# A two-layer hybrid decoder on one core: small fp32 products issued in groups, HGRN's score rows kept twice

## The chip, the cores and the metric

The kernel runs on one core of a Trainium2 chip. The metric is device time in microseconds (us) of one execution, the median over runs. Engines are named as in the profile: PE is TensorE, with PEld its weight loads, DVE is VectorE, ACT is ScalarE, POOL is GpSimd, SP is SyncE.

## The reference

One inference step of a decoder with two layers, width 1024, over 512 prompt tokens and 8 sequences of 8 sample tokens, all in fp32. A layer normalises `x`, projects it with one matrix (1024 to 2820 columns), and feeds four mixers of 256 columns each:

- SSD: a Mamba-2 mixer with 4 heads, 2 groups, state 64, and a short convolution ahead of it
- attention over a sliding window of 128 with sinks and a relative bias, 4 heads on 2 KV heads
- HGRN2: gated linear attention, 4 heads of 64 by 64
- RG-LRU: a gated linear recurrence with a convolution

```python
mix = concat([y_ssd, y_swa, y_hg, y_lru])
x = x + mix @ w_out
x = x + square(relu(rmsnorm(x) @ w_up)) @ w_down
```

The step returns the normalised `x` and all new caches and states of both groups.

## The kernel before

Activations lie transposed, features on partitions and all 576 tokens on the free axis. The big products (projections `pi`, output projection `pd`, MLP `pu`, `p`, `pd`, `pl`) split each fp32 operand into a high and a low fp32r part and run three matmuls of 128 by 128 by 288 where one would do in exact arithmetic. They stand on lines 339, 1102 and 1255. Each takes three of the eight PSUM banks (`mm`); all small products share the other five (`mx`, function `bank`).

Inside the mixers the products are small and plain fp32. One of these is issued as two matmul instructions, a transpose as one. The trace gives the part of the array that an instruction uses, as 128\*128 or 128\*64. The small products that matter here are these:

- `sc` and `scs` (lines 554 and 568): the scores of HGRN. Within a chunk of 128 tokens they are built level by level, for half lengths 1, 2, 4 up to 64 (`LEVELS`). A level scales rows of keys into `kE` and of queries into `qE` on DVE, multiplies them on PE (four `sc` for the prompt; one `scs` for the samples in the three shortest levels), and copies what its mask allows into `A` with two predicated copies for each bank. `kE` and `qE` are one buffer each. `hgrn` runs twice in each layer, for two pairs of heads.
- `dtt` (line 685): fifteen small transposes of SSD's dt values into one bank.
- `su` and `sus` (lines 781 and 793): SSD's state updates, four for the prompt's chunks and one for the samples, for each of two groups.
- `pts` (line 954): eight transposes of the sample tokens' attention weights.
- `lg`, `pt`, `ao` (lines 978, 1002, 354): the four prompt blocks of attention. A block computes scores (`lg`, four products), adds bias and takes the maximum on DVE, takes exponentials on ACT, and then, head by head, scales a row on ACT and transposes it (`pt`; 4 in the first block, 8 in the others). Two heads share a bank, which ACT copies into `PT`. The values follow (`ao`, 4 products in the first block, 8 in the others).

The four blocks are generators with three steps (scores, softmax, transposes and values), run by `staggered`, so that scores of a block are traced ahead of the transposes of the block before.

The order on each engine is set when the kernel is built: a scheduler walks the traced instructions, puts those first that were traced first among those ready by its own estimates, and raises marked ones (weight splits, what empties PSUM) over all others. `issue_after(ins)` adds an order edge on one engine and no semaphore. Each engine then works through its queue in that order. While a mixer's chain is on DVE and ACT, PE is given big products of what was traced later: projections of the next mixer, then the output projection, which for its first half (`outproj(0)`) needs HGRN and SSD, for its second (`outproj(1)`) LRU and attention.

Of the kernel before, what the change touches and what calls it, by code (L numbers as in the profile page):

```python
# [2 lines left out]

# [10 lines left out]
AF = mybir.ActivationFunctionType  # L14
# [121 lines left out]


def staggered(parts):

    n = 0  # L140
    while parts:
        n += 1
        for p in parts[:n]:
            if next(p, True):
                parts.remove(p)
                n -= 1


class Kern:
# [205 lines left out]

    def silu(self, out, in_):
        return self.nc.scalar.activation(out, in_, AF.Silu)
# [123 lines left out]
    def hgrn_begin(self):  # L481
# [3 lines left out]
        self.kE = P.t("kE")  # L485
        self.qE = P.t("qE", [2, TH])
        for t in (self.A, self.kE, self.qE):
            self.nc.gpsimd.memset(t, 0.0)
# [6 lines left out]
    def hgrn(self, p):  # L495
        nc, V, S, li, P = self.nc, self.nc.vector, self.nc.scalar, self.li, self.hp
        A, kE, qE = self.A, self.kE, self.qE
# [34 lines left out]

        for n, h in enumerate(LEVELS):
            W = T if h <= 4 else NP_
# [16 lines left out]
            ps = self.bank("sc")  # L551
            pv = ps.rearrange("p (d n) -> p d n", d=2)
            for ci in range(4):
                nc.tensor.matmul(pv[:, :, 64 * ci : 64 * ci + 64], kE[:, 128 * ci : 128 * ci + 128],  # L554
                                 qE[:, :, 64 * ci : 64 * ci + 64], start=True, stop=True)

            def into(rows, c0, c1, m, ps):
                w = (c1 - c0) // (2 * h)
# [4 lines left out]

            into(128, 0, NP_, self.lmask[:, n], pv)
            if h <= 4:
                ps = self.bank("scs")
                pv = ps[:64, :64].rearrange("p (d n) -> p d n", d=2)
                nc.tensor.matmul(pv, kE[:, NP_:T], qE[:, :, 256:288], start=True, stop=True)
                into(64, NP_, T, self.lmask[:64, n, :32], pv)
# [80 lines left out]
    def ssd_dt(self):  # L650
# [30 lines left out]
        pv = p2[:, :60].rearrange("p (c w h) -> p c w h", c=5, w=3)  # L681
        for ci in range(5):
            n = 128 if ci < 4 else NS
            for w, t in enumerate((dt, ac, ed)):
                nc.tensor.transpose(pv[:n, ci, w], t[:, 128 * ci : 128 * ci + n], self.ident[:4, :4])
# [16 lines left out]
    def ssd(self):  # L702
# [34 lines left out]
        for g in range(2):  # L737
# [39 lines left out]

            for ci in range(4):
                a = slice(128 * ci, 128 * ci + 128)
                pu = self.bank("su")  # L780
                nc.tensor.matmul(pu[rg, :128], Bt[:, 128 * ci + 64 * g : 128 * ci + 64 * g + 64], xd[:, a], start=True, stop=True)
# [6 lines left out]
            S0 = P.t("S0", [NB, 64])  # L788
# [606 lines left out]
```

## Time and profile before

| | |
|---|---|
| Median of 3 runs | 1359.47 us (1356.86, 1359.47, 1362.58) |
| The profiled execution | 1355.2 us |
| Its span on the core | 1353.4 us |
| Busy share of PE, DVE, ACT, POOL | 98%, 76%, 49%, 5% |
| Chain that ended last, by engine | PE 86%, DVE 7%, ACT 3%, issue 2% |
| Granted clock of PE, mean over the span | 0.998 |

The span runs from the first to the last instruction of the program; the execution's own time has 1.8 us around it. Times within the span are counted from its start. The mixers of the first layer lie between 0 and some 272 us, its MLP from there to 680, the second layer behind it. A matmul's end in the trace is modelled and matmuls overlap in the array, so that what one costs is read from the distance between starts, not from its duration.

### The profile page before, as it was taken

To read this page: it belongs to the slowest core of one execution; us is meant where nothing else is said; L and a number is where in the kernel's file an instruction comes from. 1 tells how busy PE (TensorE), PEld (TensorE's weight loads), DVE (VectorE), ACT (ScalarE), POOL (GpSimd) and SP (SyncE) were. 2 spreads that over 40 slices of the span, in tenths; PEclk is the share of its full clock that TensorE was granted. 3 is DMA by queue.
4 is the path that set the end of the run, shared out by engine and by line. 5 is a ranking of instruction groups with operands and counts; after the bars stand their busy time and mean duration, and the time that the engine had idled before them with its cause. 6 is when DMAs were issued, how large, how long until landed. Compare 5 with 4: busy or idle time off the path is not lost.

```text
span 1353.4 us, 25452 instructions
## 1 busy us (share of the span) xinstructions
PE 1328.0 (98%) x10384; PEld 1279.6 (95%) x10384; DVE 1028.5 (76%) x2043; ACT 658.2 (49%) x1175; POOL 63.3 (5%) x126
## 2 busy tenths in 40 slices
PE   7999999999999999999999999999999999999997
PEld 7999899799999999999999998988999999999997
DVE  7788888488678677776669678886977677777755
ACT  6565436766243334333354774477653243334325
POOL 2201102000000000000000001100000000000000
PEclk9999999999999999999999999999999999999999
DMA  6324414123213222322331233231223213222312
GB/s 237 104 87 139 165 68 144 48 79 110 77 65 110 78 92 81 113 75 86 131 121 47 98 117 128 94 111 48 79 81 123 78 63 109 79 82 91 115 58 71
DMA packets 39831, 131.36 MB, mean 97 GB/s; under 512 B 6089, under 2 KB 8241, under 8 KB 39681
## 3 DMA queue, kind: packets, MB, share of 16 engines
q1 hardware_dynamic: 29312, 102.12, 21.9%
q0 software_dynamic: 6512, 22.64, 5.0%
q10 hardware_dynamic: 3888, 4.97, 1.2%
q8 instruction: 82, 1.34, 0.4%
q14 instruction: 37, 0.30, 0.1%
HBM read 120.32 MB, written 11.34 MB: 97 GB/s over the span
## 4 chain that ended last, share of the span: by engine, by line
PE 86%; DVE 7%; ACT 3%; issue 2%; DMA 0%; SPq 0%; DVEq 0%; ACTq 0%
PE pd L339 33%; PE p L1102 21%; PE pi L339 15%; PE pu L339 6%; PE pl L1255 2%; PE sc L554 2%; DVE lo L326 1%; DVE a L444 1%; PE ss L402 1%; PE ao L354 1%; ACT hi L326 1%; DVE A L562 1%; DVE qE L550 1%; PE y L354 1%; PE lg L978 1%
## 5 line engine op out<-in xcount | busy, mean ns | idle before, releaser
L326 ACT CAST hi<-raw 128x1024 fp32r<-128x1024 f32 x134 | 140.2, 1046 | 297.1 <-PE pd L339 144.6
L339 PE MATMUL pd<-fh,hi 128*128 128x288 f32 x960 | 284.1, 296 | 0.0
L339 PE MATMUL pd<-fl,hi 128*128 128x288 f32 x960 | 284.0, 296 | 0.0
L339 PE MATMUL pd<-fh,lo 128*128 128x288 f32 x960 | 282.8, 295 | 0.0
L339 PE MATMUL pi<-xh,hi 128*128 128x288 f32 x704 | 210.6, 300 | 7.6 <-ACT xh L377 7.1
L339 PE MATMUL pi<-xl,hi 128*128 128x288 f32 x704 | 210.4, 300 | 1.1 <-DVE xl L378 1.1
L339 PE MATMUL pi<-xh,lo 128*128 128x288 f32 x704 | 211.1, 300 | 0.0
L326 DVE TENSOR_TENSOR lo<-raw,hi 128x1024 fp32r<-128x1024 f32 x134 | 163.6, 1222 | 27.3 <-ACT hi L326 26.7
L1037 DVE TENSOR_TENSOR x<-x,pd 128x288 f32<-128x288 f32 x240 | 108.2, 451 | 97.9 <-PE pd L339 97.8
L339 PEld LDWEIGHTS pd<-fh,lo 128*128 128x128 f32 x960 | 180.9, 188 | 0.0
L339 PEld LDWEIGHTS pd<-fh,hi 128*128 128x128 f32 x960 | 180.4, 188 | 0.0
L339 PEld LDWEIGHTS pd<-fl,hi 128*128 128x128 f32 x960 | 180.4, 188 | 0.0
L339 PEld LDWEIGHTS pi<-xh,hi 128*128 128x128 f32 x704 | 133.0, 189 | 10.1 <-ACT xh L377 7.1
L339 PEld LDWEIGHTS pi<-xh,lo 128*128 128x128 f32 x704 | 132.9, 189 | 6.0 <-issue 5.2
L339 PEld LDWEIGHTS pi<-xl,hi 128*128 128x128 f32 x704 | 132.9, 189 | 3.6 <-DVE xl L378 1.7
L1102 PE MATMUL p<-Th,ul 128*128 128x288 f32 x312 | 92.2, 296 | 0.0
L1102 PE MATMUL p<-Tl,uh 128*128 128x288 f32 x312 | 92.1, 295 | 0.0
L1102 PE MATMUL p<-Th,uh 128*128 128x288 f32 x312 | 92.0, 295 | 0.0
L1102 PE MATMUL p<-xl,uh 128*128 128x288 f32 x312 | 91.9, 295 | 0.0
L1102 PE MATMUL p<-xh,ul 128*128 128x288 f32 x312 | 91.9, 295 | 0.0
L1102 PE MATMUL p<-xh,uh 128*128 128x288 f32 x312 | 91.7, 294 | 0.0
L1078 ACT CAST uh<-raw 128x1024 fp32r<-128x1024 f32 x52 | 54.5, 1048 | 66.8 <-PE p L1102 43.2
(489 smaller groups left out, 3003.2 us busy)
## 6 DMA issues: line engine op xcount, KB each, us to landing
raw<-in_wu SPq DMA_DIRECT2D x64, 512.0 KB, 3.3
raw<-in_wd SPq DMA_DIRECT2D x64, 512.0 KB, 4.2
raw<-in_wi SPq DMA_DIRECT2D x44, 512.0 KB, 3.3
raw<-in_wo SPq DMA_DIRECT2D x16, 512.0 KB, 3.2
x<-in_xT SPq DMA_DIRECT2D x8, 288.0 KB, 5.9
a<-acd ACTq DMA_DIRECT2D x4, 576.0 KB, 4.5
xl<-in_xT POOLq DMA_DIRECT2D x8, 288.0 KB, 4.3
xd<-x POOLq DMA_DIRECT2D x8, 288.0 KB, 2.4
```

Of the source, the lines that this page charges most:

```text
L326: self.split_ins = nc.scalar.copy(hi, raw).ins, nc.vector.tensor_tensor(lo, raw, hi.bitcast(F32), op=ALU.subtract).ins
L339: self.nc.tensor.matmul(out, w, x[:, a], start=n == 0, stop=n == last)
L354: self.nc.tensor.matmul(out, w, x, start=n < 2, stop=n >= len(products) - 2, skip_group_check=True)
L402: nc.tensor.matmul(ps[:, :TH], ones, s[:, TH * h : TH * h + TH], start=n == 0, stop=n == len(sqs) - 1)
L444: V.scalar_tensor_tensor(dst[:, :CW], src[:, k : k + CW], w(k), dst[:, :CW], op0=ALU.mult, op1=ALU.add)
L550: V.tensor_tensor(qE[r, d, : W // 2].rearrange("p (n h) -> p n h", h=h), qu[r], eu[r], op=ALU.mult)
L554: nc.tensor.matmul(pv[:, :, 64 * ci : 64 * ci + 64], kE[:, 128 * ci : 128 * ci + 128], qE[:, :, 64 * ci : 64 * ci + 64], start=True, stop= ...
L562: V.copy_predicated(Av[:, d], m, ps[:, d].rearrange("p (n h) -> p n h", h=h))
L1037: self.nc.vector.tensor_tensor(y[:, a], x[:, a], ps, op=ALU.add)
L1078: S.copy(hl[0], src)
L1102: nc.tensor.matmul(ps[:, :TH], u, x, start=j == 0, stop=j == 11)
L1255: nc.tensor.matmul(ps, u[:, o + q], v[:, a], start=j == 0, stop=j == 11)
```

## The change

Instructions are regrouped; the arithmetic stays as it is. A helper, `together`, issues a list of products and puts an order edge from the first one to all the others on PE. The list is turned round, so that the first is one whose input is traced last. The 15 `dtt`, the 8 `pts` and each block's `pt` go through it.

HGRN gets two buffers each of `kE` and `qE`, all cleared at the start. Levels are held in pairs and a pair's products are issued together, the later level first; the seventh level stands alone. The predicated copies follow for both.

In SSD the samples' update `sus`, with its state load and the spreading of B by sequence ahead of it, moves in front of the four `su`, which stand behind it by an order edge.

In attention the blocks are four plain functions in a written order instead of generators. All four heads are scaled before the block's transposes. The values of a block are traced after the transposes of the next block and behind the first of these by an order edge; so are the scores of the block after the next. `PT` has four buffers instead of three, since a block's two live longer.

```diff
 
+    def together(self, calls):
+
+        first = calls[0]().ins
+        with self.tc.issue_after(first):
+            for c in calls[1:]:
+                c()
+        return first
...
         self.A = P.t("A", [2, T])
-        self.kE = P.t("kE")
-        self.qE = P.t("qE", [2, TH])
-        for t in (self.A, self.kE, self.qE):
+        self.kE = [P.t("kE", bufs=2) for i in range(2)]
+        self.qE = [P.t("qE", [2, TH], bufs=2) for i in range(2)]
+        for t in (self.A, *self.kE, *self.qE):
             self.nc.gpsimd.memset(t, 0.0)
...
 
+        held = []
         for n, h in enumerate(LEVELS):
+            kE, qE = self.kE[n % 2], self.qE[n % 2]
...
                 V.tensor_tensor(qE[r, d, : W // 2].rearrange("p (n h) -> p n h", h=h), qu[r], eu[r], op=ALU.mult)
-            ps = self.bank("sc")
-            pv = ps.rearrange("p (d n) -> p d n", d=2)
-            for ci in range(4):
-                nc.tensor.matmul(pv[:, :, 64 * ci : 64 * ci + 64], kE[:, 128 * ci : 128 * ci + 128],
-                                 qE[:, :, 64 * ci : 64 * ci + 64], start=True, stop=True)
-
-            def into(rows, c0, c1, m, ps):
-                w = (c1 - c0) // (2 * h)
+            held.append((n, h, kE, qE))
+            if n % 2 == 0 and h < LEVELS[-1]:
+                continue
+
+            first, banks = None, []
+            for n, h, kE, qE in held[::-1]:
+                ps = self.bank("sc")
+                banks.append((128, 0, NP_, h, self.lmask[:, n], ps.rearrange("p (d n) -> p d n", d=2)))
+                pv = banks[-1][-1]
+                for ci in range(4):
+                    with self.tc.issue_after(first) if first else nullcontext():
+                        ins = nc.tensor.matmul(pv[:, :, 64 * ci : 64 * ci + 64], kE[:, 128 * ci : 128 * ci + 128],
+                                               qE[:, :, 64 * ci : 64 * ci + 64], start=True, stop=True).ins
+                    first = first or ins
+                if h <= 4:
+                    ps = self.bank("scs")
+                    banks.append((64, NP_, T, h, self.lmask[:64, n, :32], ps[:64, :64].rearrange("p (d n) -> p d n", d=2)))
+                    with self.tc.issue_after(first):
+                        nc.tensor.matmul(banks[-1][-1], kE[:, NP_:T], qE[:, :, 256:288], start=True, stop=True)
+            held = []
+            for rows, c0, c1, h, m, ps in banks:
                 m = m.rearrange("p (n h) -> p n h", h=h)
                 Av = A[:rows, :, c0:c1].rearrange("p d (n u h) -> p d n u h", u=2, h=h)[:, :, :, 1]
                 for d in range(2):
                     V.copy_predicated(Av[:, d], m, ps[:, d].rearrange("p (n h) -> p n h", h=h))
-
-            into(128, 0, NP_, self.lmask[:, n], pv)
-            if h <= 4:
-                ps = self.bank("scs")
-                pv = ps[:64, :64].rearrange("p (d n) -> p d n", d=2)
-                nc.tensor.matmul(pv, kE[:, NP_:T], qE[:, :, 256:288], start=True, stop=True)
-                into(64, NP_, T, self.lmask[:64, n, :32], pv)
...
         pv = p2[:, :60].rearrange("p (c w h) -> p c w h", c=5, w=3)
+        calls = []
         for ci in range(5):
             n = 128 if ci < 4 else NS
             for w, t in enumerate((dt, ac, ed)):
-                nc.tensor.transpose(pv[:n, ci, w], t[:, 128 * ci : 128 * ci + n], self.ident[:4, :4])
+                calls.append(partial(nc.tensor.transpose, pv[:n, ci, w], t[:, 128 * ci : 128 * ci + n], self.ident[:4, :4]))
+        self.together(calls[::-1])
...
 
+            S0 = P.t("S0", [NB, 64])
+            self.dma(S0, self.I["sS0"][li, :, g])
+            ve = P.t("b", SLOT, bufs=2)
+            self.by_sequence(ve, Bt[:64, NP_ + 64 * g : NP_ + 64 * g + 64])
+            ps = self.bank("sus")
+            first = nc.tensor.matmul(ps, xd[:64, NP_:640], ve[:64, :512], start=True, stop=True).ins
             for ci in range(4):
                 a = slice(128 * ci, 128 * ci + 128)
                 pu = self.bank("su")
-                nc.tensor.matmul(pu[rg, :128], Bt[:, 128 * ci + 64 * g : 128 * ci + 64 * g + 64], xd[:, a], start=True, stop=True)
+                with self.tc.issue_after(first):
+                    nc.tensor.matmul(pu[rg, :128], Bt[:, 128 * ci + 64 * g : 128 * ci + 64 * g + 64], xd[:, a], start=True, stop=True)
                 if ci == 0:
                     V.tensor_copy(new[ci][rg], pu[rg, :128].rearrange("p (j n) -> p j n", j=2))
                     continue
                 for j in range(2):
                     V.scalar_tensor_tensor(new[ci][rg, j], new[ci - 1][rg, j], self.el[rg, j, ci : ci + 1],
                                            pu[rg, 64 * j : 64 * j + 64], op0=ALU.mult, op1=ALU.add)
-            S0 = P.t("S0", [NB, 64])
-            self.dma(S0, self.I["sS0"][li, :, g])
-            ve = P.t("b", SLOT, bufs=2)
-            self.by_sequence(ve, Bt[:64, NP_ + 64 * g : NP_ + 64 * g + 64])
-            ps = self.bank("sus")
-            nc.tensor.matmul(ps, xd[:64, NP_:640], ve[:64, :512], start=True, stop=True)
...
                 S.activation(l, l, AF.Copy, scale=sm[:, i, u : u + 1])
-        pc, pn = P.t("PT", [2, 256], bufs=3), P.t("PT", [2, 256], bufs=3)
-        for dst, rows, a in ((pc, 128, slice(0, 128)), (pn, 64, slice(128, 192))):
-            ps = self.bank("pts")
-            for k in range(4):
-                nc.tensor.transpose(ps[:rows, 128 * k : 128 * k + 128], Ls[k // 2][:, k % 2, a], self.ident)
+        pc, pn = P.t("PT", [2, 256], bufs=4), P.t("PT", [2, 256], bufs=4)
+        parts = [(self.bank("pts"), *x) for x in ((pc, 128, slice(0, 128)), (pn, 64, slice(128, 192)))]
+        self.together([partial(nc.tensor.transpose, ps[:rows, 128 * k : 128 * k + 128], Ls[k // 2][:, k % 2, a], self.ident)
+                       for ps, dst, rows, a in parts for k in (3, 2, 1, 0)])
+        for ps, dst, rows, a in parts:
             S.copy(dst[:rows].rearrange("p a n -> p (a n)"), ps[:rows])
...
 
-        def block(nb):
+        def scores(nb, behind=None):
             s0, n = (128 * (nb - 1), 256) if nb else (0, 128)
-            nk = n // 128
             a = slice(128 * nb, 128 * nb + 128)
             L = [P.t("L", [2, 256], bufs=4) for _ in range(2)]
-            mx, sm, ng = (self.small([128, 4], c) for c in ("mx", "sm", "ng"))
+            mx = self.small([128, 4], "mx")
             lg = [self.bank("lg").rearrange("p (e n) -> p e n", e=2) for i in range(2)]
-            for e in range(2):
-                for i in range(2):
-                    nc.tensor.matmul(lg[i][:, e, :n], Q[e][kv(i), a], K[kv(i), s0 : s0 + n], start=True, stop=True)
+            with self.tc.issue_after(behind) if behind else nullcontext():
+                for e in range(2):
+                    for i in range(2):
+                        nc.tensor.matmul(lg[i][:, e, :n], Q[e][kv(i), a], K[kv(i), s0 : s0 + n], start=True, stop=True)
             for i in range(2):
                 for e in range(2):
                     h = 2 * i + e
                     V.tensor_tensor_reduce(out=L[i][:, e, :n], in0=lg[i][:, e, :n], in1=bias[:, h, 256 - n :], scale=1.0,
                                            scalar=sinks[:, h : h + 1], op0=ALU.add, op1=ALU.max, accum_out=mx[:, h : h + 1])
-            yield
+            return L, mx, s0, n, a
+
+        def softmax(L, mx, s0, n, a):
+            sm, ng = (self.small([128, 4], c) for c in ("sm", "ng"))
             V.tensor_scalar(ng, mx, -1.0, None, op0=ALU.mult)
...
             V.tensor_tensor(sm, sm, mx, op=ALU.add)
             V.reciprocal(sm, sm)
-            yield
-            PT = [P.t("PT", [2, 256], bufs=3) for _ in range(2)]
-            for i in range(2):
-                pt = self.bank("pt").rearrange("p (e n) -> p e n", e=2)
-                for e in range(2):
-                    h = 2 * i + e
-                    l = L[i][:, e, :n]
-                    S.activation(l, l, AF.Copy, scale=sm[:, h : h + 1])
-                    for k in range(nk):
-                        nc.tensor.transpose(pt[:, e, 128 * k : 128 * k + 128], l[:, 128 * k : 128 * k + 128], self.ident)
-                S.copy(PT[i][:, :, :n], pt[:, :, :n])
+            for h in range(4):
+                l = L[h // 2][:, h % 2, :n]
+                S.activation(l, l, AF.Copy, scale=sm[:, h : h + 1])
+
+        def turned(L, mx, s0, n, a):
+            PT = [P.t("PT", [2, 256], bufs=4) for _ in range(2)]
+            pt = [self.bank("pt").rearrange("p (e n) -> p e n", e=2) for i in range(2)]
+            first = self.together([partial(nc.tensor.transpose, pt[i][:, e, 128 * k : 128 * k + 128],
+                                           L[i][:, e, 128 * k : 128 * k + 128], self.ident)
+                                   for i in (1, 0) for e in (1, 0) for k in range(n // 128)])
+            for i in (1, 0):
+                S.copy(PT[i][:, :, :n], pt[i][:, :, :n])
+            return first, PT
+
+        def values(PT, s0, n, a, behind=None):
             po = self.bank("ao").rearrange("p (e n) -> p e n", e=2)[:, :, :128]
             at = lambda i, k: s0 + 128 * k + 64 * i
-            self.tiled([(po[kv(i), e], vt[:, at(i, k) : at(i, k) + 64], PT[i][:, e, 128 * k : 128 * k + 128])
-                        for k in range(nk) for e in range(2) for i in range(2)])
+            with self.tc.issue_after(behind) if behind else nullcontext():
+                self.tiled([(po[kv(i), e], vt[:, at(i, k) : at(i, k) + 64], PT[i][:, e, 128 * k : 128 * k + 128])
+                            for k in range(n // 128) for e in range(2) for i in range(2)])
             S.copy(oh[:, :, a], po)
             V.tensor_tensor(ol[:, :, a], po, oh.bitcast(F32)[:, :, a], op=ALU.subtract)
 
-        staggered([block(nb) for nb in range(4)])
+
+        blocks = [scores(0), scores(1)]
+        softmax(*blocks[0])
+        old = None
+        for nb in range(4):
+            first, PT = turned(*blocks[nb])
+            if old:
+                values(*old, first)
+            if nb < 3:
+                softmax(*blocks[nb + 1])
+            if nb < 2:
+                blocks.append(scores(nb + 2, first))
+            old = PT, *blocks[nb][2:]
+        values(*old)
```

## Rows read from the trace of the kernel before

**Rows 1.** The page, busy time: engine, us busy, share of the span, instructions.

```profile
PE 1328.0 (98%) x10384; PEld 1279.6 (95%) x10384; DVE 1028.5 (76%) x2043; ACT 658.2 (49%) x1175; POOL 63.3 (5%) x126
```

**Rows 2.** Busy time by stretch: stretch, its length, engines' busy time, PEclk, DMA.

```profile
302.50:689.80 387.30, 387.30 (x2919) 387.06 (x2918) 287.61 (x519) 155.56 (x260) 8.73 (x16) 1.00 0.28 96
243.84:271.71 27.87, 26.62 (x199) 21.77 (x197) 14.39 (x58) 21.27 (x67) 0.00 (x0) 1.00 0.11 39
```

**Rows 3.** Waits of PE, whole span: us in total, times, longest us.

```profile
PE pts L954 <- ACT L L949: 1.6, 2, 1.3
PE pt L1002 <- ACT L L1000: 1.6, 2, 0.8
```

**Rows 4.** Timeline of PE, one short HGRN level, layer 1: start us, us, operation.

```profile
837.60 0.29 PE L339 MATMUL pi<-xh,lo 128*128 128x288 f32 x1
837.81 1.13 PE L554 MATMUL sc<-qE,kE 128*128 128x128 f32 x8
838.87 0.33 PE L568 MATMUL scs<-qE,kE 128*64 128x64 f32 x2
839.13 0.40 PE L339 MATMUL pi<-xh,hi 128*128 128x288 f32 x1
839.37 0.29 PE L339 MATMUL pi<-xl,hi 128*128 128x288 f32 x1
```

**Rows 5.** Timeline of PE, attention's prompt blocks, layer 0.

```profile
250.21 0.28 PE L1002 MATMUL pt<-cst,L 128*128 128x128 f32 x1
...
250.46 0.29 PE L1002 MATMUL pt<-cst,L 128*128 128x128 f32 x1
...
250.81 0.43 PE L354 MATMUL ao<-PT,vt 128*64 128x128 f32 x2
...
253.44 0.66 PE L1002 MATMUL pt<-cst,L 128*128 128x128 f32 x4
...
254.20 0.60 PE L1002 MATMUL pt<-cst,L 128*128 128x128 f32 x4
254.76 0.43 PE L354 MATMUL ao<-PT,vt 128*64 128x128 f32 x2
255.13 0.40 PE L339 MATMUL pd<-mixh,hi 128*128 128x288 f32 x1
255.46 0.70 PE L978 MATMUL lg<-x,x 64*128 64x256 f32 x2
256.08 1.09 PE L354 MATMUL ao<-PT,vt 128*64 128x128 f32 x14
257.10 1.13 PE L978 MATMUL lg<-x,x 64*128 64x256 f32 x6
258.16 0.40 PE L339 MATMUL pd<-mixl,hi 128*128 128x288 f32 x1
```

**Rows 6.** Timeline of PE, SSD's states, layer 1.

```profile
792.45 0.29 PE L339 MATMUL pi<-xl,hi 128*128 128x288 f32 x1
792.67 1.09 PE L781 MATMUL su<-c,Bt 128*64 128x128 f32 x8
793.69 0.40 PE L339 MATMUL pi<-xh,lo 128*128 128x288 f32 x1
...
795.08 1.12 PE L793 MATMUL sus<-b,c 64*128 64x512 f32 x2
796.13 0.40 PE L339 MATMUL pi<-xh,lo 128*128 128x288 f32 x1
```

**Rows 7.** Timeline of PE, a dt transpose, layer 1.

```profile
762.05 0.22 PE L685 MATMUL dtt<-cst,b 4*128 4x4 f32 x1
762.20 0.40 PE L339 MATMUL pi<-xh,hi 128*128 128x288 f32 x1
```

**Rows 8.** Timeline of POOL, the start.

```profile
1.74 0.58 POOL L488 MEMSET kE<- 128x576 f32 x1
...
11.86 0.84 POOL L208 COPY gate<-x 128x1 f32<-128x1 f32 x1 [8.52 <-DMA x<-in_xT]
```

More of the change, by code (lines that the diff above doesn't have):

```diff
@@ L2 @@
 from contextlib import ExitStack, nullcontext
+from functools import partial
 import numpy as np
@@ L135, in seqs @@
     return t[:, o : o + NB * w].rearrange("p (b t) -> p b t", b=NB)
[L138 to L146, printed above, removed]
 class Kern:
@@ L496, in hgrn @@
         nc, V, S, li, P = self.nc, self.nc.vector, self.nc.scalar, self.li, self.hp
-        A, kE, qE = self.A, self.kE, self.qE
+        A = self.A
         f, v, q, g = self.hin
```

## The prediction

> **What bounds the kernel.** I read the page first: TensorE is busy 98% of the span [rows 1]. A busy TensorE says little, since its matmuls overlap, so the next view is busy time by stretch. In the MLP of the first layer 2919 big products take 387.30 us, 0.1327 us from one start to the next, at a granted clock of 1.00 [rows 2]; nothing there is edited. In the four prompt blocks of the first layer's attention the same engine is busy 26.62 of 27.87 us, while ScalarE is busy 21.27 [rows 2]. The view of waits then shows how little of this is waiting: 1.6 us in all before the sample transposes (`pts`) and 1.6 us before the prompt transposes (`pt`), both for ScalarE's scaled rows [rows 3]. So the kernel is TensorE's issue stream from end to end. An edit is worth what it takes out of that stream, as long as the chain of softmax work does not turn the time into waits. The timeline shows where the stream is bad: not in the number of fp32 products, which is the same after, but in what one costs beside its neighbours. I read it by start-to-start distances and not by durations, because the ends are modelled.
>
> **The price of a neighbour.** One fp32 product is two instructions, called halves here; a transpose is one. A lone transpose between two big products: from one `pt` to the next is 0.25 us with one big product between them [rows 5], less 0.13 for the big one, 0.12. Four in a row take 0.56 us up to the next kind, 0.14 each, with the change of shape at their end in it [rows 5]. Both work on the tile 128\*128, as the big products do. Where the shape changes it is dear: `su` (tile 128\*64) starts 0.22 us after the last big product, its last half holds the next big product back [rows 6], and the big product after an `scs` needs 0.24 instead of 0.13 until its successor starts [rows 4]. So a group of another shape costs about 0.09 at its entry and 0.11 at its exit, and its own first and last halves are stretched too.
>
> The Trainium skill, TensorEngine Tiling (Array Packing), Key Properties, states it as a rule: a change of tiling mode drains TensorE, a change of tile alone does not. The trace agrees: 0.12 us for the lone transpose in the same mode, 0.22 us of entry into another mode. The rule speaks against a good part of this edit, since transposes (`pt`, `pts`) and the HGRN scores (`sc`) have the mode of the big products; by it their grouping is worth nothing, and without it, at the drain's price for each group, some 7 us more would be had.
>
> **The change part by part.**
>
> *Attention, prompt blocks.* The same 28 transposes, 56 value halves and 32 score halves a layer. Grouping the transposes gains nothing by the lone price; I take 0, bounds 0 and 0.5 us in all. What it brings is that the values of a block no longer stand behind the copies of their own block, half of which are late. Before, a burst goes two value halves, one big product, two score halves, fourteen value halves, six score halves: 3.40 us from 254.76 to 258.16 [rows 5], 3.27 without the big product. Unbroken, sixteen value halves cost the 1.02 of fourteen plus one step of about 0.11, and eight score halves the 1.06 of six plus about 0.21 (over a sixth of it, since the two halves of a pair start together), 2.40 together; fully paired, without the odd half at each end, 2.08. The gain is 0.87 to 1.19; I take 1.0. The first block's burst of eight and eight takes 2.63 [rows 5]; the same pieces unbroken make 0.65 (eight at the 0.073 of the fourteen and a longer first step) and 1.27, gain 0.7, or 1.0 paired; I take 0.8. Each occurs once in each layer: 3.6 us. In three of the other four blocks the values are broken only by big products, as two, a big one, fourteen: 0.37 for two halves that cost 0.11 in a run and 0.33 for a big product that costs 0.13 [rows 5], 0.46 lost, 1.4 us for three. Attention together 5.0, bounds 3.5 and 6.5.
>
> *HGRN scores.* Seven levels become four groups, in four calls: twelve groups fewer. A short level (`sc` and `scs`) costs 1.77 us from the last big product before it to the second behind it [rows 4], 1.50 without two big ones. In a pair, the second loses its entry (0.21 against 0.13: 0.08) and an exit (0.11), but `scs` now stands before an `sc`, and the way back into 128\*128 costs about 0.05 more than in a run: 0.13. Pairs with one `scs` or none save the entry alone, 0.08. Per call 0.13 + 0.08 + 0.08, for four calls 1.2 us; bounds 0 (the shape changes are as many) and 2.3 (entry and exit for all twelve). The vector work is unchanged. A level's rows wait for the pair before last instead of the last level, but DVE then stops behind both levels' scores at once; the big projections that fill TensorE meanwhile hide this, and without them it would cost DVE some 1 us a pair.
>
> *SSD states.* `su` costs 0.22 + 1.02 + 0.24 less two big ones, 1.21; `sus` 0.22 + 1.05 + 0.24 − 0.27 = 1.24 [rows 4, 6]. Joined, one entry and one exit: 2.26, gain 0.19. Four of these, and in one the four `su` are split today, about 0.3 more: 1.0 us, bounds 0.4 and 1.4. The state load and DVE's spreading of B move ahead; the same instructions, and DVE is not the bound here.
>
> *dt transposes.* Lone, one costs 0.22 + 0.15 + 0.24 − 0.27 = 0.34 [rows 4, 6, 7], in a run I put it at 0.06, under half of its own 0.15. Four stand apart today, two of them beside other fp32 products: 0.9 us, bounds 0 and 1.1.
>
> *Rows kept twice.* Two more clears of 0.58 us on POOL a layer [rows 8]. In the first, POOL sits idle 8.52 us before the gate copy [rows 8], which hides them; without that they would delay the first loads by 1.2. Two copies of the larger buffers move addresses; I count 0.
>
> The sum is 5.0 + 1.2 + 1.0 + 0.9 = 8.1 us, bounds 3.9 and 11.3.
>
> **What comes back as waits.** The first of each group is the one that is ready last: ten groups of transposes (two `pts`, eight `pt`) now stand on TensorE's queue behind the scaling of all heads, and everything behind them stands too: other transposes, the last block's values, the next scores, the big products. Today such waits add up to 3.2 us in four [rows 3]. Values a block late also make the output projection's second half begin a block later. Below, waits could vanish (−3.2); above, ten of the longest of either kind, 1.3 us [rows 3], 13. I take 2.0 more than today, about one wait of 0.8 to 1.3 in each layer. ScalarE sets a floor: 21.27 us of work in the stage, 6.6 below its length [rows 2], so a gain of 2.5 in it fits.
>
> 8.1 − 2.0 = 6.1 us from the profiled execution's 1355.2 us (span 1353.4 and 1.8 around it) gives 1349.1. The median of the three runs is 1359.47, 4.3 above that execution, so the forecast for a median is 1353.4 us.
>
> **The rivals.**
>
> *The softmax chain takes it.* TensorE saves 8.1 but waits for ScalarE nearly as long. For it: every idle stretch of TensorE in attention ends on ScalarE [rows 3], which is busy for three quarters of the stage [rows 2]. Against: it also waits for TensorE's broken bursts, which end sooner. With waits of 5 to 8 us: 1356.5 to 1359.5. Chance 0.23.
>
> *Slower.* The place is the head of each transpose group. It decides from 0.8 us of wait per group (ten of these are the 8.1). At 1.3, the longest today, the sum is 13 − 8.1 = 4.9 more, 1364.4; at 1.6, 1367.4. For it: both kinds of wait exist today with only one or two heads awaited. Against: the scheduler has big products to put ahead. Chance 0.12, two thirds of it past the bound below.
>
> *Any group costs, whatever its shape.* Then 35 fewer groups (18 `pt`, 5 `pts`, 12 `sc`) save more: at the 0.08 of a late entry 2.8, at a full entry and exit of 0.20 7.0: 1350.6 to 1346.4; vanished waits lead the same way. For it: lone products often show the 0.21 entry [rows 4]. Against: the lone transpose at 0.12. By the page's rule named above it would not happen. Chance 0.20.
>
> *The change does not do what it says.* An order edge puts the rest behind the first, not next to it; big products may still come between. Then only the dt and SSD parts count: about 1357.6. Against: the big products near these groups are traced later and so rank lower. Chance 0.05.
>
> **How the numbers follow.** The forecast, 1350.5 to 1356.5, has 0.40. What a measurement of this kernel can tell from no change is about 0.5%, 6.8 us: faster means under 1352.7, slower over 1366.3. Half the forecast and all of "any group costs" lie under: 0.40. Two thirds of "slower" lie over: 0.08. The rest, 0.52, is within. The range, from the lower of the "any group" times, with a little of the vanished waits, to the "slower" case at a wait of about 1.2 a group: 1345.5 to 1363.5. The forecast alone is 1350.5 to 1356.5.
>
> **What the profile after would show.** Right: in attention, sixteen value halves without a break in about 1.0 to 1.1 us, directly behind eight transposes, scores in one piece; stage times of 24 to 26 us at the same number of big products; `su` directly behind `sus`; about half as many stretches of fp32. Wrong: new waits of TensorE on ScalarE's scaled rows in the view of waits, above all before `pt`; fewer big products left at the end of a layer with idle TensorE before the last values; fp32 stretches still split; `sc` pairs that wait for DVE or for PSUM banks, since a pair of short levels holds four of the five small banks.

## The result, and the profile after

The changed kernel is slower: 1377.67 us (median of 5, 1374.65 to 1380.62) against 1356.89 (median of 5), a ratio of 1.0147, interval 1.0122 to 1.0173. The forecast was 1353.4, the range ended at 1363.5. The profiled execution after has a span of 1374.8 us, 21.4 more than before.

The page after, busy time and the granted clock in 40 slices of the span:

```profile
PE 1335.8 (97%) x10384; PEld 1287.9 (94%) x10384; DVE 1026.9 (75%) x2043; ACT 659.6 (48%) x1175; POOL 64.7 (5%) x130
...
PEclk9999699999999999999999999998999999999999
```

TensorE does the same 10384 instructions as in [rows 1] and is busy 7.8 us longer. Two slices show a fallen clock, the fifth (layer 0's SSD) and the twenty-eighth (layer 1's attention); a third fall, in layer 0's attention, is too short for its slice and shows in the stretches below. The waits of TensorE after (us in total, times, longest), to be held against [rows 3]:

```profile
PE pt L348 <- ACT L L1007: 11.8, 6, 3.8
PE pi L329 <- ACT xh L375: 7.5, 1, 7.5
PE sus L791 <- DVE c L784: 5.0, 2, 4.2
PE pts L348 <- ACT L L958: 2.2, 2, 1.1
```

Waits before the prompt transposes have grown by 10.2 us, and `sus` has one of 4.2 us that is new; the 7.5 us are the start of the program, 7.1 to 7.9 us in every variant here. The stretches in question, after: stretch, length, busy PE, PEld, DVE, ACT, POOL, then the granted clock as a share of 2.4 GHz, and the DMA (a count can hold a neighbour that reaches into the stretch):

```profile
148.38:170.80 22.42, 21.41 (x109) 15.35 (x110) 13.44 (x36) 8.17 (x20) 3.43 (x6) 0.51 0.22 71
272.11:283.29 11.18, 7.41 (x64) 6.50 (x65) 1.45 (x7) 6.74 (x19) 0.00 (x0) 0.69 0.15 47
937.17:952.66 15.49, 8.92 (x70) 7.46 (x68) 3.58 (x17) 9.87 (x30) 0.00 (x0) 0.67 0.03 13
```

The first is an unbroken chain of small products in SSD, from `sus` to HGRN's first scores, at the lower of the clock's two levels. Before, 99 of these halves stand in one chain too, in 10.60 us at full clock:

```profile
148.61:159.21 10.60, 9.73 (x99) 7.52 (x99) 7.93 (x22) 6.01 (x13) 1.95 (x4) 1.00 0.32 107
```

The other two are the end of attention in layers 0 and 1. In layer 1 the timeline of TensorE reads:

```profile
937.54 0.29 PE L329 MATMUL pd<-mixh,lo 128*128 128x288 f32 x1
941.13 0.33 PE L348 MATMUL pt<-cst,L 128*128 128x128 f32 x1 [3.30 <-ACT L L1007]
941.29 1.23 PE L351 MATMUL pt<-cst,L 128*128 128x128 f32 x7
942.46 1.98 PE L344 MATMUL ao<-PT,vt 128*64 128x128 f32 x16
947.71 0.47 PE L348 MATMUL pt<-cst,L 128*128 128x128 f32 x1 [3.27 <-ACT L L1007]
947.97 1.70 PE L351 MATMUL pt<-cst,L 128*128 128x128 f32 x7
949.60 3.12 PE L344 MATMUL ao<-PT,vt 128*64 128x128 f32 x32
952.66 0.40 PE L329 MATMUL pd<-mixh,hi 128*128 128x288 f32 x1
```

The groups are as the change wants them: eight transposes, sixteen values, no big product inside. But none is left *between* them either, so ScalarE's scaling of four rows, at 3.3 us a time, lies open.

**Where the 21.4 us are.** With each big product taken at the 0.1327 us of [rows 2], the time beside them says which stage lost: from layer 0's dt transposes to the samples' attention scores `ls` 12.5 us; from the samples' attention values `aos` to the sums of squares ahead of the MLP 2.3 in layer 0 and 5.4 in layer 1; nothing else moved by over 1. (The first expectation below takes 0.1247 a product, which moves none of these by more than 0.5.)

### The profile page after: what moved, and what is told of

Its sections match the earlier page's. It is cut to its first block, busy times and chain, and to the rows that moved or that the text cites. A ratio compares the mean times of both kernels' runs of the same rounds, so it can differ in the third digit from the quotient of the medians.

```text
span 1374.8 us, 25437 instructions
## 1 busy us (share of the span) xinstructions
PE 1335.8 (97%) x10384; PEld 1287.9 (94%) x10384; DVE 1026.9 (75%) x2043; ACT 659.6 (48%) x1175; POOL 64.7 (5%) x130
## 4 chain that ended last, share of the span: by engine, by line
PE 89%; DVE 5%; ACT 4%; issue 1%; DMA 1%; ACTq 0%; DVEq 0%
PE pd L329 33%; PE p L1132 21%; PE pi L329 16%; PE pu L329 6%; PE sc L562 2%; PE pl L1285 2%; PE ss L400 1%; ACT L L1007 1%; ACT hi L316 1%; PE y L344 1%; DVE L L991 1%; DVE lo L316 1%; PE ao L344 1%; ACT L L1000 1%; PE lg L860 1%
## 5 line engine op out<-in xcount | busy, mean ns | idle before, releaser
L329 PEld LDWEIGHTS pi<-xh,hi 128*128 128x128 f32 x704 | 132.9, 189 | 10.2 <-ACT xh L375 7.5
```

Source lines behind the costliest of these rows:

```text
L329: self.nc.tensor.matmul(out, w, x[:, a], start=n == 0, stop=n == last)
```

## The experiments

The quoted text ahead of each result is what was expected of the run. Theory A at first: `sus` at the head of SSD's states waits for VectorE and halves the clock behind it (12 us), and attention's end lacks big products (7 us). Its rivals, B in the texts below: the other groups used up SSD's big products; attention only suffered from a clock that had fallen elsewhere. All were timed beside the kernel before on their chip (median 1356.4 to 1357.1); intervals are of the ratio to it.

### One part undone, or one part alone

```
ssd_undone     su, then the state load, B's spreading and sus, as before
att_undone     prompt blocks as before
both_undone    both
att_only       the kernel before with the new prompt blocks, nothing else
```

> The change but for SSD's states: as before, the four prompt products su ahead of sus, with the state load and the spreading of B behind them. Time less big products at a nominal 0.1247 us each grew in layer 0 from the dt transposes to the attention's ls by 12 us, and in the attention (aos to the MLP's ss) by 2.2 us in layer 0 and 5.1 us in layer 1. Theory A (sus at the head of PE waits 4.2 us for the sample part of xd, and the clock halves behind it): those 12 us come back, 1364 to 1368 us against 1377.7, and no half clock in layer 0's SSD. Rival B (the groups of the dt transposes and of the HGRN scores used up the big products that lay between SSD's steps; 8 are left ahead of group 1 either way): the long unbroken chain stays, so does the half clock, 1373 to 1378 us.

Measured 1375.12 [1.0107, 1.0153]: 2.5 us come back, not 12. The wait for `sus` is gone, but a wait of the same size for VectorE now stands before SSD's output `y`, and the half clock stays: 109 small halves in 24.38 us. Theory A is wrong for SSD.

```profile
PE y L344 <- DVE a L766: 4.5, 1, 4.5
```

> The change but for the attention's blocks, which are written as before (the query block of the sample part stays grouped). Theory A (no big products between the last two blocks, and PE waits for ScalarE's scaling in both layers): 7 us come back, 1369 to 1372 us, and layer 1's half clock goes; layer 0's SSD stays as in the changed kernel. Rival B (the attention is no slower by itself, its tail only shows a clock that fell for another reason): within 2 us of 1377.7.

Measured 1367.51 [1.0050, 1.0094]: 10.2 us come back, more than theory A's 7, and far from rival B. The half clock of layer 1's attention goes, that of layer 0's SSD stays.

> SSD's states and the attention's blocks as before; HGRN's pairs of levels, the dt transposes and the sample part's transposes grouped. Theory A: 19 us come back and the little that these three groups save shows, 1355 to 1360 us. Rival B (these groups take big products away from SSD's chain in layer 0): layer 0 still loses 8 to 12 us, 1364 to 1370 us.

Measured 1365.26 [1.0035, 1.0078]: rival B. With SSD and attention's blocks untouched, layer 0 still has its chain of 109.

> The kernel before with the attention's blocks alone as in the change. Theory A: the 7 us of the attention's tail alone, 1362 to 1366 us, with waits of 2 to 4 us at pt3 ahead of ao16 in both layers. Rival B: 1354 to 1358 us, for the groups save what was predicted and the tail was slow only by a fallen clock.

Measured 1366.52 [1.0042, 1.0097], 10.0 over before and 0.5 above theory A's range: attention loses by itself. Its waits of TensorE:

```profile
PE pt L348 <- ACT L L996: 14.0, 8, 3.5
```

### What used up SSD's big products

The trace shows layer 0's dt transposes at 118.2 us after, at 108.4 to 115.9 before, though HGRN's first half ends 7 us *sooner* (its state update `u` at 86.3, not 93.5) and `pdt`, the product from which dt comes, stands at 93.9, not 99.9. ScalarE between them, after (L669 to L671 are dt's absolute value, exponential and logarithm):

```profile
99.78 0.67 ACT L669 ACTIVATE b<-b 4x576 f32<-4x576 f32 x1
100.47 1.28 ACT L355 ACT_TABLE_LOAD   x1
101.76 0.26 ACT L355 ACTIVATE X<-a 128x64 f32<-128x64 f32 x1
102.04 1.28 ACT L360 ACT_TABLE_LOAD   x1
103.33 1.05 ACT L316 CAST hi<-raw 128x1024 fp32r<-128x1024 f32 x1
104.29 0.67 ACT L457 CAST mixh<-o 128x576 fp32r<-128x576 f32 x1
104.86 0.68 ACT L670 ACTIVATE b<-b 4x576 f32<-4x576 f32 x1
105.56 1.28 ACT L355 ACT_TABLE_LOAD   x1
106.85 1.17 ACT L355 ACTIVATE z<-z 128x1152 f32<-128x1152 f32 x1
108.04 1.28 ACT L360 ACT_TABLE_LOAD   x1
109.55 1.05 ACT L316 CAST hi<-raw 128x1024 fp32r<-128x1024 f32 x1 [0.22 <-PE pi L329]
110.50 0.77 ACT L671 ACTIVATE b<-b,c 4x576 f32<-4x576 f32 x1
```

and the same three operations in the kernel before:

```profile
104.42 0.68 ACT L663 ACTIVATE b<-b 4x576 f32<-4x576 f32 x1
...
105.58 0.67 ACT L664 ACTIVATE b<-b 4x576 f32<-4x576 f32 x1
...
106.73 0.76 ACT L665 ACTIVATE b<-b,c 4x576 f32<-4x576 f32 x1
```

From the first to the third it is 2.31 us before and 10.72 after, because SSD's silus (L355) now come into it, each with a load of its function table (1.28 us) and one back; before, they stood ahead of it. Theory C: HGRN's pairs end sooner, ScalarE's order turns over, dt is late; TensorE fills the time with in-projections. Ahead of SSD's second group only 8 are then left, and none behind its states, where 20 and 34 stood before; the small products run in one chain.

```
hgrn_only   before + rows kept twice + pairs of levels
dtt_only    before + dt transposes in one group
both_dt     both_undone, and in the function that computes dt
            + with self.tc.high_priority(HP):
                  pdt, dt, abs, exp, ln, scan, ed   (the chain up to its exp)
after_dt    the changed kernel with the same line
dt_alone    before with the same line
hgrn_dt     hgrn_only with the same line
```

> The kernel before with HGRN's rows kept twice and its levels in pairs, nothing else. Theory C: HGRN's first half ends 6 us sooner (87 against 94 us in the traces), so ScalarE takes up SSD's silus before the dt chain is through; each switch of its function table is 1.28 us, the dt chain from pdt to the dt transposes grows from 8.5 to 24 us (to the first, 14 to 24 us to the last), TensorE fills that time with in-projections, and SSD's chain of small products behind it finds none left: one unbroken chain of 109 halves at half clock in layer 0. Then this part alone costs some 8 to 10 us: 1364 to 1368 us. Rival D (the delay is the grouping of the dt transposes, which makes the first wait for the last): within 3 us of before, 1354 to 1359 us.

Measured 1369.56 [1.0062, 1.0105], 13.2 us lost, and more than expected. Its SSD chain:

```profile
145.84:169.18 23.34, 18.67 (x109) 13.60 (x110) 15.49 (x39) 9.13 (x21) 3.44 (x6) 0.63 0.21 68
```

> The kernel before with the fifteen dt transposes in one group, nothing else. Theory C: within 2 us of before (1355 to 1358 us), since big products still lie between SSD's steps. Rival D: 6 us or more are lost here, 1363 us and above.

Measured 1356.13 [0.9982, 1.0003]: rival D is out.

> As both_undone (SSD's states and attention blocks as before, HGRN's pairs, dt and sample transposes grouped), with the dt chain (pdt to the exponential ed) at high priority, so that no silu comes into it. Theory C: the 8.8 us that both_undone is over the kernel before go, 1353 to 1357 us, no half clock in layer 0's SSD, 90 to 115 big products between the dt transposes and the last y. Rival E (the clock falls because the pairs leave less big work around SSD in any case): 1361 us or more.

Measured 1354.49 [0.9971, 0.9990], 10.8 us under both_undone. ScalarE's chain, and SSD's:

```profile
97.24 0.67 ACT L670 ACTIVATE b<-b 4x576 f32<-4x576 f32 x1
...
100.15 0.68 ACT L671 ACTIVATE b<-b 4x576 f32<-4x576 f32 x1
...
102.72 0.78 ACT L672 ACTIVATE b<-b,c 4x576 f32<-4x576 f32 x1
```

```profile
147.61:158.38 10.77, 10.00 (x100) 7.44 (x100) 10.09 (x27) 6.49 (x15) 2.90 (x5) 1.00 0.23 75
```

5.48 us instead of 10.72, dt transposes at 108.6, a chain of 99 at full clock, with 20 big products ahead of SSD's second group and 22 behind its states. Theory C holds; its count was off, for 179 big products lie between the dt transposes and the last `y`, not 90 to 115.

> The changed kernel with the dt chain at high priority, nothing else. Theory C: 9 to 12 us come back, 1365 to 1369 us, and what is left over the kernel before is the attention's 10 us. Rival F (SSD's states product sus at the head costs its wait wherever it stands): 1372 us or more.

Measured 1365.95 [1.0040, 1.0080]: 11.7 us come back in the changed kernel, as theory C had it and not rival F.

> The kernel before with the dt chain at high priority, nothing else. Theory C (the priority cures a displacement that this kernel does not have): within 1.5 us of before, 1355 to 1358 us. Rival I (the priority is worth 8 us or more by itself): 1349 us or less.

Measured 1361.92 [1.0026, 1.0054], 4.8 us *slower*: the priority is no gain of its own. This lies outside what both sides expected: it too shifts the order, and layer 1's attention shows a new chain of 56 halves in 11.22 us. Its profiled execution, one of the three at 1363.6 to 1365.0 (the other three took 1359.9 to 1360.3), also had a granted clock of 0.51 behind layer 0's dt transposes, from 111.65 to 122.00. The priority cures what the pairs displace and upsets an order that had no such fault.

> The kernel before with HGRN's pairs of levels and the dt chain at high priority, nothing else. Theory C: 12 to 15 us under hgrn_only's 1369.6, 1354 to 1357 us; what it lies under dt_alone is the pairs' own worth, predicted as 1.2 us. Rival E (the pairs lose in any case): 1361 us or more.

Inconclusive as a time: two executions gave 1354.81 and 1357.64 us, two more 2606, at a clock shown as full, which nothing here explains and which are left out. The two, one inside theory C's range and one 0.6 above it, speak for theory C and not for rival E.

### What costs in attention

TensorE's order in the two kernels shows what the values' new place does. `outproj(1)`, the half of the output projection that needs LRU and attention, works on 288 columns at a time, and its products for columns 0 to 287 need blocks 0 to 2 alone. Before, block 2's values stood ahead of block 3's transposes, and 21 big products of it filled block 3's waits (153 came after the last values). With the values held `behind` block 3's transposes, all 174 come after.

```
att_mend_only = att_only, att_mend = both_dt + new prompt blocks, and in both
+            if nb == 3: values(*old)
             first, PT = turned(*blocks[nb])
-            if old: values(*old, first)
+            if old and nb < 3: values(*old, first)
att_mendh = att_mend, a block's transposes in head order without together(),
            values and scores behind the last of them instead of the first
```

> The kernel before with the attention's blocks as in the change (no other part), but block 2's values are issued ahead of block 3's transposes and not behind them. Theory G: the first half of the last out-projections needs blocks 0 to 2 alone; with the values held behind the next transposes, 21 products of it come behind block 3 and none are left for the last two waits. Moved ahead, 12 to 18 of them lie ahead of block 3: layer 0 loses nothing any more and layer 1 keeps one wait of 3 us; 1358 to 1362 us against 1366.5 with the values behind. Rival H (it is the grouping of a block's transposes, which wait for all four scaled rows): 1364 us or more.

Measured 1356.85 [0.9995, 1.0018]: 9.7 of att_only's 10.0 us are gone by moving one block's values, more than expected. Theory G. The profiled execution took 1363.09 us, the nine others 1355.01 to 1359.03: SSD's chain, in exactly the order of the kernel before, had the lower clock there, in 15.9 us instead of 10.6.

```profile
149.86:165.78 15.92, 15.92 (x99) 12.06 (x99) 10.08 (x28) 6.35 (x16) 1.96 (x4) 0.57 0.32 105
```

> As both_dt (dt chain at high priority, SSD's states as before), with the attention's blocks grouped as in the change and block 2's values ahead of block 3's transposes. Theory G: no wait but the last of some 2 us in either layer, 1353 to 1358 us beside both_dt's 1354.5. Rival H: 1360 us or more.

Measured 1353.28 [0.9967, 0.9987], theory G's time, but not its waits: TensorE still waits more than before for the head of a group:

```profile
PE pt L348 <- ACT L L1007: 6.8, 6, 2.1
```

> As att_mend, but a block's transposes go head by head and not in one group; scores and values stay in one piece. Theory G: within 2 us of att_mend. Rival H: 3 us or more below att_mend, 1352 to 1356 us.

Measured 1350.90 [0.9949, 0.9971], 2.4 us under att_mend, between the two expectations: rival H is right by that much, and wrong as the main cause. The profiled execution took 1355.74 us, the six others 1350.24 to 1351.30; the difference is a clock fallen in SSD's chain, in the order that ran at full clock in both_dt:

```profile
147.36:163.30 15.94, 15.94 (x100) 11.97 (x100) 12.82 (x35) 7.26 (x19) 2.89 (x5) 0.57 0.26 83
```

### SSD's states, and all parts mended

```
ssd_dt         both_dt + SSD's states as in the change (sus, then four su)
ssd_su_first   ssd_dt, four su and then sus, still tied; loads and B's spreading as in the change
best2          all parts: dt priority, su then sus, block 2's values first, transposes head by head
```

> As both_dt, with SSD's states as in the change (sus ahead of the four su); attention's blocks as before. If sus at the head costs only where no big products are ahead of it (33 to 42 are, here): 1353 to 1356.5 us beside both_dt's 1354.5. Rival F (its wait for the sample part costs wherever it stands): 1357 us or more.

Measured 1358.79 [1.0005, 1.0024], 4.3 over both_dt (3.9 if each is held against the kernel before on its chip): rival F, which after_dt had seemed to rule out.

> As ssd_dt (1358.8 us), but the four su go first and sus last, still tied together; the state load and the spreading of B stay ahead on VectorE. If sus at the head is what costs: 1354 to 1356 us, as both_dt. If the order on VectorE is: 1357.5 to 1360 us.

Measured 1354.64 [0.9969, 0.9988], as both_dt: the order on VectorE costs nothing. The edges did not bring `su` and `sus` together here: three of the four groups have big products between them, the same three as in both_dt. With `sus` at the head it stands directly ahead of `su` in all four (in two of them the last `su` is apart). So the two runs do not tell `sus` at the head from the join itself.

Of the price, 1.8 us is one wait that ssd_dt and after_dt have and both_dt and ssd_su_first do not: behind layer 0's SSD chain a projection waits for the VectorE operation that writes `x` (`sus` itself waits 0.8 us in all in ssd_dt):

```profile
PE pi L329 <- DVE x L417: 1.8, 1, 1.8
```

By stages (with 0.1327 us a big product, as above) ssd_dt is 2.0 us over both_dt from layer 0's dt transposes to its `ls`, 1.6 over it in the same stage of layer 1, 0.7 under it from `ls` to `aos` in each layer, and 1.0 and 1.3 over it from there to the MLP. Several runs of small products are cut otherwise there (`lg` as 8 and 8, `y` and `ys` interleaved in layer 1). How the one leads to the other stays open.

> All parts of the change with three mends: the dt chain at high priority, su ahead of sus, block 2's values ahead of block 3's transposes, and transposes head by head. Theories C and G together: 1350 to 1354 us, under the kernel before; where the chain of 99 halves in layer 0 runs at half clock in an execution, 5 us more.

Measured 1350.61 [0.9939, 0.9968]: 0.47% under the kernel before, and the fastest here, with att_mendh within 0.3 us of it. Its page, and its waits:

```profile
PE 1322.9 (98%) x10384; PEld 1277.3 (95%) x10384; DVE 1026.1 (76%) x2043; ACT 658.0 (49%) x1174; POOL 65.3 (5%) x130
```

```profile
PE pts L348 <- ACT L L961: 2.0, 2, 1.0
PE pt L1015 <- ACT L L1010: 1.9, 2, 1.1
```

5.1 us less of busy TensorE than [rows 1], with waits about those of [rows 3].

## Why the prediction was wrong

Three steps of it failed: the 2.0 us for waits, resting on big products that the scheduler would put ahead; the taking of other engines' order as fixed; and the clock, which is in no term. What TensorE saves came out near the forecast, in part by luck.

**The price of a neighbour.** The stretches of small products, counted as unbroken runs of their starts, go from 122 before to 74 after and 79 in att_mend, with 1672 halves each time. In att_mend, at full clock, they take 146.62 us with 13.37 of waiting, before 151.54 with 7.95: net of waits 133.25 against 143.59. Big products net of waits take 2.5 more. That is 7.9 us saved, where the same parts (all but SSD's states) were forecast at 7.1. The parts are not as forecast, though. From `aos` to the MLP, with 320 big products and at full clock in each of these kernels:

| | Length, layers 0 and 1 | Of it waits | Stretches in a layer |
|---|---|---|---|
| both_dt | 61.28, 60.99 us | 1.55, 1.26 us | 20 |
| att_mendh | 59.16, 58.87 us | 1.69, 1.39 us | 16 |
| att_mend | 60.29, 60.01 us | 4.04, 3.78 us | 6 |

Net of waits attention saves 7.0 us of TensorE in att_mend, past its bound of 6.5, and 0.9 is left for HGRN and the dt and sample groups, where 2.1 were forecast. That the sum fits is two misses that nearly cancel.

**Attention, 5.0.** ssd_su_first to best2 changes the prompt blocks alone, with block 2's values moved and the transposes head by head: 4.0 us. By the table, values and scores in one piece save 4.5 net of waits, and grouping the transposes saves another 2.5, where it was put at 0 to 0.5; but the waits of the groups take 4.7, so that grouping loses 2.3 there and 2.4 by the medians. So the head of a group was the right place for a loss, as the rival "Slower" said, but its size there is a quarter of attention's 10.0. The step that failed is the sentence against that rival, "the scheduler has big products to put ahead". The prediction noticed that values a block late delay the output projection's second half (`outproj(1)`) and charged nothing for it. The products of it that blocks 0 to 2 release were the filler of the last waits: 9.7 us over two layers.

**HGRN, 1.2.** The failed step is the taking of the rest as fixed: "The vector work is unchanged", and big projections "fill TensorE meanwhile". Both look at two engines and at what is done, not at when. A first half that ends 7 us sooner met a ScalarE whose order then put SSD's silus into the dt chain; the projections were used up while dt was late, and the pairs cost 13.2 us alone. No rival had this. The pairs' own worth could not be timed apart; together with the dt and sample groups, and the priority, it is 1.9 us (both_dt), where 2.1 were forecast. This tests the term little, since the priority alone moves the kernel before by 4.8 us the other way.

**SSD states, 1.0.** Wrong in sign: some 4 us lost with `sus` at the head, and with the four `su` first the time of both_dt within error, but hardly any join. The joined group takes 2.07 us; `su` and `sus` apart take 1.02 and 1.05 in both_dt, the same, so what a join saves lies at most at the big products around it. The sentence that VectorE is not the bound passed over the fact that a group waits for the latest operand of its first member. In the changed kernel that is the sample part of `xd`, queued on VectorE behind an operation that waits for a DMA, where `su` needs only the prompt part:

```profile
146.55 1.29 DVE L759 TENSOR_TENSOR a<-a,dtt 128x512 f32<-128x512 f32 x2 [1.57 <-DMA a<-acd]
147.76 0.28 DVE L761 TENSOR_TENSOR a<-a,dtt 64x128 f32<-64x128 f32 x1
...
147.96 0.28 DVE L784 TENSOR_TENSOR c<-c,dtt 64x128 f32<-64x128 f32 x1
...
148.38 2.04 PE L791 MATMUL sus<-b,c 64*128 64x512 f32 x2 [4.18 <-DVE c L784]
```

**dt transposes, 0.9.** Measured 0.2, within error of nothing, inside 0 to 1.1; the profiled execution of dtt_only had a granted clock of 0.73 from 115.7 to 122.0, so that the grouping's worth at full clock may be more. **Rows kept twice, 0:** not timed apart; nothing in the profiles speaks against it.

**Waits, 2.0.** The term counts the heads of the ten transpose groups. They waited 3.2 us in all before and 14.0 after (11.8 and 2.2), so 10.8 more: five times what was taken, though inside the bound of 13. That bound priced each at 1.3, the longest of a kernel that still had filler; the longest after is 3.8. `sus` adds 5.0 that no term held. In all stretches of small products the waits grew by 14.4 us (7.95 to 22.34).

**The rivals.** "Slower" had the size of the waits about right at 1.3 a group, and its 1364.4 still ends 13 us short of the measured time: it has no clock in it either. "Any group costs, whatever its shape" is right in one pair of runs: between att_mendh and att_mend ten stretches a layer go, most of them transposes on the big products' own tile, and 2.5 us with the twenty, some 0.12 each. By the rule that the prediction weighed (the Trainium skill, TensorEngine Tiling (Array Packing), Key Properties: only a change of mode drains) these would be worth nothing. Here the measurement decides against that use of it. The trace of the kernel before shows the same: behind an `sc` that ends on the tile 128\*128, the first big product needs 0.22 us until its successor starts, the next one 0.13:

```profile
724.44 1.13 PE L554 MATMUL sc<-qE,kE 128*128 128x128 f32 x8
725.33 0.38 PE L339 MATMUL pi<-xh,lo 128*128 128x288 f32 x1
725.55 0.29 PE L339 MATMUL pi<-xh,hi 128*128 128x288 f32 x1
725.68 0.30 PE L339 MATMUL pi<-xl,hi 128*128 128x288 f32 x1
```

The prediction's "The trace agrees" rests on the lone transposes alone; [rows 4] already had 0.21 ahead of `sc`.

**The clock.** In no term. Net of waits the stretches of small products take 147.38 us in the changed kernel (169.72 less 22.34) and 133.25 in att_mend, at full clock with the same halves: some 14 us, an estimate of what the lower level costs, as much as the waits. Undone one by one, the parts give back 10.2 us (attention) and 2.5 (SSD's order), both together 12.4, and both_undone is still 8.8 over the kernel before: together about the 20.8. HGRN's pairs alone cost 13.2, more than these 8.8; no run shows why they cost less beside the dt and sample groups.

**The signs.** Of those for a wrong forecast, new waits before `pt` and an idle TensorE ahead of the last values came true; of those for a right one, fewer stretches did.

## What to carry to other kernels

Big products that depend on nothing recent are a stock, and every wait of the small chain draws on it: before an edit of the order, count how many lie ahead of each wait and ask which edit releases them. A result that comes sooner is an edit of the order too, on every engine whose order is built from what is ready first. When grouping, look for the member with the latest operand, since at the head it makes the whole group wait, and keep ahead of the last wait whatever releases the next big work. A sum that comes out near can hide two misses: hold the parts against rows as well.

## What the runs showed of the hardware

The chain of 99 small halves in layer 0's SSD ran at full clock in 10.77 us (both_dt) and at 0.57 in 15.94 (att_mendh): 5.2 us for the same work, in different executions. TensorE's order is the same in both up to the end of the chain, instruction by instruction. The order of the kernel before did both as well: 10.60 us at 1.00 in its own profile, 15.92 at 0.57 in att_mend_only's. With ten halves more ahead of it and waits of 4 to 5 us inside or ahead, it ran at 0.51 to 0.63 in each of the profiled executions of the changed kernel, ssd_undone, both_undone and hgrn_only. What decides between the two levels in a given execution stays open.

A run of small products costs at its end even on the big products' own tile: 0.22 us instead of 0.13 for the first big product behind it. A switch of ScalarE's function table took 1.28 us each time.
